# A streaming encoder step: gate and z projections in pairs by seven block products, in a stage of their own

## Chip, cores and metric

The kernel runs on one core of a Trainium2 chip. The metric is device time in microseconds of one launch, inputs and outputs in device memory. One core has five engines that each run their own list of instructions in program order: TensorE (PE, matrix products into PSUM), VectorE (DVE), ScalarE (ACT), GpSimd (POOL) and SyncE (SP, which issues most transfers).

## What is computed

One layer of an encoder for 512 prompt tokens and 64 sample tokens (576 columns in all), width 2048, fp32. Cut to what matters:

```python
h = RMSNorm(x) * (1 + scale) + shift
[gdn q|k|v, gdn z, gdn beta, gdn a, att q, att k, att v, att z,
 idx q, idx k, idx w, gate_a, gate_b] = h @ W_in
A = W_bA( GatedRMSNorm(GatedDeltaRule(silu(conv4(qkv)))) * silu(z_A) )
B = W_bB( SparseAttn_topk(indexer) * silu(z_B) )
x = x + gate * W_out( sigmoid(gate_a) * A + sigmoid(gate_b) * B )
```

The delta rule has 16 heads of 128 x 128 state, walked in chunks of 64 tokens with a triangular solve per chunk. The indexer scores keys for each token, and only the 256 best take part in the attention (16 heads, 2 key heads, 1024 cached keys for the sample). Outputs are y, the new keys, values and indexer keys, and the new delta-rule and convolution states.

## The kernel before

**Tiles.** Almost all of PE's time goes into the products of h (576 columns, held on chip, transposed, as a high part `hh` and a low part `hl`) with weight matrices, 128 weight columns at a time. Such a *tile* takes 96 matmuls: 16 blocks of the inner dimension, two halves of 288 tokens, and three products each (high x high, high x low, low x high) that together stand for one fp32 product. These are the matmuls with a 128x288 operand, here called wide. `run_tile` and `half` (L292) run one. While tile n runs, `load` (L261) brings the weights of tile n+3 by one 1 MB transfer of SP, and `split` (L273) makes the high part of tile n+1's weights (`whi`, a copy on ACT) and the low part (`wlo`: ACT writes the negated high part, and a transfer of POOL's queue adds the raw weights to it). At the end of each half a tile's epilogue runs: for a gate tile tanh on ACT (`gth`, `gate_epi` L1459) and a store to device memory (`d_t`); for a z tile tanh and a product on DVE (`gz`, `za_epi` L1512) and a store (`d_za`).

**Order.** `plan` (L1668) writes the list of tiles. Everything else (convolution, solve, scan, attention, top-k) is written as generators, the *tasks*. While the program is built, `tick` follows each matmul and lets the tasks that are due put in their next instructions; due times come from a book-keeping of the engines in the planner. So tasks' instructions lie between those of the tiles, and each engine's list is fixed when the kernel is built. A tile may have a function to run ahead of it (`pre`): `q_pre(h)` (L1237) does `join` on the scan of head h-2, `qb_pre` (L1408) joins attention tasks, and `open_gdn`, `open_att`, `open_ga` change the memory pools and join what is left. A `join` puts in all the instructions of a task up to its end with no tile matmul between them.

**Stages.** Keys kb0, kb1, then `misc` (indexer keys, beta, a), eight indexer-query tiles qi0 to qi7 with the score products, values vb0 and vb1, seven gates g00 to g06 during which DVE does the top-k (`topks` L886: 16 rounds each for three prompt blocks, 32 rounds for the sample, one MAX8 and one MATCH_REPLACE per round). Then the delta rule: for each head tiles c0, c1, c2 (its q, k, v; c02 is q of head 2) with 12 z tiles and 9 gates among them, 4.3 tiles per head in the mean. Per head: convolution (`conv` L912), products kk, steps on M (`solve` L1059; the block `dN` goes through a transfer first), products z and y, then the scan (`scan` L1146) with state S and products pks, px, pS, po, a norm on DVE, and transposes oTp, oTq of the result ot. Three more gates, then 16 pairs of tiles qb, zb with attention (`attend` L1306), two gates after zb7, four z tiles, eight gates g18 to g115 under which `load_ga` brings oa and za from device memory (`ga<-oa`), then the branch products ya, yb and wo.

Of the kernel before, what the change touches and what calls it, by code (L numbers as in the profile page):

```python
# [16 lines left out]
D = 2048  # L17
KO = 16
# [9 lines left out]
MARK = -3e38  # L28


O_QA, O_ZA, O_BA, O_QB, O_KB, O_VB, O_ZB, O_QI, O_KI, O_GA, O_GB = (
# [174 lines left out]
class Kern(Plan):  # L206
# [51 lines left out]
    def win(self, name, c, epi, pre=None, n=128):  # L258
        self.add(name, [(self.i["w_in"][0], c, n)], lambda: self.h, epi, pre)

    def load(self, n):  # L261
        if n >= len(self.stream):
# [4 lines left out]
        r3 = raw[:, :KO * m].rearrange("p (k m) -> p k m", m=m)  # L267
        at = 0
        for src, c, w in d["srcs"]:
            self.S.dma_start(r3[:, :, at:at + w], src[:, c:c + w].rearrange("(k p) m -> p k m", p=128))  # L270
            at += w

    def split(self, n, q, of=4, eng=None):  # L273
        if n >= len(self.stream):
            return
        d = self.stream[n]
        if q == 0:
            d["hi"] = self.wp.tile([128, 2048], F32R, tag="whi", name=f"whi{n}")
            d["lo"] = self.wp.tile([128, 2048], F32R, tag="wlo", name=f"wlo{n}")
        w = KO * d["m"] // of  # L280
        s = slice(w * q, w * q + w)
        self.A.activation(d["hi"][:, s], d["raw"][:, s], AF.Copy)
        if eng:
            eng.tensor_tensor(d["lo"][:, s], d["raw"][:, s], d["hi"][:, s].bitcast(F32), op=ALU.subtract)
            return

        self.A.activation(d["lo"][:, s], d["hi"][:, s].bitcast(F32), AF.Copy, scale=-1.0)
        if q % 2:
            s = slice(w * q - w, w * q + w)
            self.G.dma_start(d["lo"][:, s], d["raw"][:, s], accum_op=ALU.add)  # L290

    def half(self, n, s, ps, ks, hook=None, part=None):  # L292

        d = self.stream[n]
        m = d["m"]
        hi = d["hi"][:, :KO * m].rearrange("p (k m) -> p k m", m=m)
        lo = d["lo"][:, :KO * m].rearrange("p (k m) -> p k m", m=m)
        ah, al = d["act"]()
        sl = slice(288 * s, 288 * s + 288)
        i = 0  # L300
        for k in ks:
            for j, (w, x) in enumerate(((hi, ah), (hi, al), (lo, ah))):
                if part is not None and part != j // 2:
                    continue
                self.mm(ps[:m, :288], w[:, k, :], x[:, k, sl], start=k == 0 and j == 0, stop=k == KO - 1 and j == 2)
                i += 1
                if hook:
                    hook(i)
                self.tick()

    def run_tile(self, n):
        d = self.stream[n]
        if d["pre"]:
            d["pre"]()

        count = [0]

        def hook(_):
            i = count[0] = count[0] + 1
            if i in (4, 14, 24, 34):  # L320
                self.split(n + 1, (i - 4) // 10)
            if i == 84:
                self.load(n + 3)

        ps = {}
# [17 lines left out]


    def consts(self, ctx):
# [4 lines left out]
        self.mE = cp.tile([128, 2, 128], F32, name="mE")  # L350
        self.ones = cp.tile([128, 1], F32, name="ones")
# [6 lines left out]
        dt = self.dp.tile  # L358
        self.d_g = dt([16, TX], F32, name="d_g")
        self.d_kT = dt([2, 128, T], F32, name="d_kT")  # L360
        self.d_v = dt([T, 256], F32, name="d_v")
# [77 lines left out]
    def start(self, ctx, hctx):  # L439
# [9 lines left out]
        with tc.tile_pool(name="x0", bufs=2, side="right", reuse_waits="tile") as xp:  # L449
# [16 lines left out]
            for t in range(5):  # L466
# [6 lines left out]
                    self.rows_load(xp, [s[0:96]], "s0", S), self.rows_load(xp, [s[96:144]], "s1", S)]  # L473
            S.dma_start(self.mE, i["k_mask"])
            S.dma_start(self.diag, i["k_diag"])
# [177 lines left out]
    def misc(self):  # L653
        i, o, p, A, V, G, mT = self.i, self.o, self.p1, self.A, self.V, self.G, self.mT
        cp = self.cp
        yield [mT]

        for a, b, at in ((0, TP, 0), (TP, T, TP + PAST)):
            c = slice(at, at + b - a)
            A.activation(self.kih[0:64, c], mT[0:64, a:b], AF.Copy)  # L660
            A.activation(self.kih[64:128, c], mT[0:64, a:b], AF.Copy)
            for x, R in enumerate((slice(0, 64), slice(64, 128))):
                V.tensor_tensor(self.kil[R, c] if at else self.kiz[R, x, :], mT[0:64, a:b], self.kih[0:64, c].bitcast(F32), op=ALU.subtract)
        mt = p.tile([128, 5, 112], F32, name="mt", bufs=1)
# [78 lines left out]
        yield [self.d_g]  # L743

    def cache_idx(self):
        i, p = self.i, self.p1
# [70 lines left out]
    def score(self, m, qi, qs):  # L817
# [4 lines left out]
        else:  # L822
            yield from self.wait(self.misc_task, self.cache_task)
        units = []
# [634 lines left out]
    def gate_epi(self, b, j):  # L1459
        def epi(ps, s):  # L1460
            if s == 0:
                p = self.gpool()
                n = 2 if p is self.p2 else 1
                self.room(p, n)
                self.gth = p.tile([128, T], F32, tag="gth", name=f"gth{b}{j}", bufs=n)
            th = self.gth
# [201 lines left out]
    def plan(self):  # L1668
        self.stream = []
        w = self.i["w_in"][0]  # L1670
        for which, col in (("k", O_KB), ("v", O_VB)):
            for n in range(2):
                self.win(f"{which}b{n}", col + 128 * n, self.kv_epi(which, n))
            if which == "k":
                self.add("misc", [(w, O_KI, 80), (w, O_BA, 32)], lambda: self.h, self.misc_epi)
                for m in range(8):
                    self.win(f"qi{m}", O_QI + 128 * m, self.qi_epi(m))
        gates = [(b, j) for b in range(2) for j in range(KO)]
# [14 lines left out]

        gate(1)
        gate(6, self.open_gdn)
        for h in range(H):
            for j, g in (((1, 0), ) if h == 0 else ()) + ((0, h), (2, h)) + (((1, h + 1), ) if h < 15 else ()):
                self.win(f"c{j}{g}", 2048 * j + 128 * g, self.conv_epi(j, g), (self.q_pre(g), self.head_pre(g), None)[j])
            z(1) if h % 4 else gate(1)
            if h < 4:  # L1700
                gate((3, 1, 0, 0)[h])
            if h % 4 == 3:
                gate(1)
# [21 lines left out]
    def drain(self):  # L1725
        while self.tasks:
            self.join(*self.tasks)

    def open_gdn(self):
# [3 lines left out]
        self.c2, self.p2 = self.pool("p2")  # L1733
        self.slack = 0.0
        self.gpool = lambda: self.p2
# [52 lines left out]
    def run(self):  # L1788
        tc = self.tc
        with ExitStack() as ctx:  # L1790
# [10 lines left out]
            self.score_tasks, self.topk_task = [], None  # L1801
            self.topk_gap, self.solve_gap, self.gada_gap = 100, 0, 5000
            self.plan()
            self.hctx = ExitStack()
            pss = self.start(ctx, self.hctx)
            self.catt, self.ap = self.pool("att", bufs=1)
            self.msk = [self.ap.tile([128, 128 * t + 128], F32, name=f"msk{t}") for t in range(4)]
            self.msks = self.ap.tile([128, NS], F32, name="msks")
            self.c1, self.p1 = self.pool("p1")
            self.gpool, self.p2 = lambda: self.p1, None  # L1810
            p = self.p1
            self.kih, self.kil = (p.tile([128, TP + NS], F32R, name=n, bufs=1) for n in ("kih", "kil"))

            self.kiz = p.tile([128, 2, TP], F32R, name="kiz", bufs=1)
            for x, R in enumerate((slice(64, 128), slice(0, 64))):
                self.V.tensor_scalar(self.kiz[R, x, :].rearrange("p (a b) -> p a b", b=128),
                                     self.ident[R].unsqueeze(1).to_broadcast([64, 4, 128]), 0.0, None, op0=ALU.mult)
            self.qss = []
            for b in range(2):
                q = p.tile([128, 2, 128], F32R, name=f"qss{b}", bufs=1)  # L1820
                self.V.tensor_scalar(q, self.ident.unsqueeze(1).to_broadcast([128, 2, 128]), 0.0, None, op0=ALU.mult)
                self.qss.append(q)
            self.tri = p.tile([128, 2, 128], F32, name="tri", bufs=1)
            self.cache_task = self.spawn(self.cache_idx())
            self.load(3)
# [4 lines left out]
            self.load(4)  # L1830
            for n in range(2, len(self.stream) - 2):
                self.run_tile(n)
# [63 lines left out]
```

## Time and profile before

| | us |
|---|---|
| median of three runs | 3089.07 |
| lowest and highest | 3082.39, 3091.2 |
| the profiled execution | 3076.14 |
| its span in the trace | 3074.4 |

A row of a group view gives an operation as output<-inputs, its shape, the count, busy time, the mean of one in ns, and what ended the idle time before it. In a strip, each digit is the busy share of one fortieth of the span in tenths. A row of a timeline gives start, duration, engine, line, operation, count and, in brackets, the idle time before it and what released it. The granted clock (PEclk) is given as a share of full speed, 2.4 GHz.

### The profile page before, as it was taken

How to read it: one execution, taken by the hardware profiler on the slowest of the kernel's cores; microseconds unless marked ns; L12 is line 12 of the kernel's file. 1: busy time of each engine (PE TensorE's matmuls, PEld its weight loads, DVE VectorE, ACT ScalarE, POOL GpSimd, SP SyncE). 2: the span in 40 equal slices, each digit the busy share in tenths (PEclk: the TensorE clock that was granted, in tenths of full speed). 3: DMA queues.
4: the chain of work that ended last, by engine and by line, in shares of the span. 5: the costliest groups of instructions: out<-in, count | busy, mean ns of one | idle time of the engine just before them, and what ended most of it. 6: DMA issues, size and time to landing. Idle time of an engine off the chain costs nothing.

```text
span 3074.4 us, 56422 instructions
## 1 busy us (share of the span) xinstructions
PE 2949.8 (96%) x22363; PEld 2811.9 (91%) x22363; DVE 1389.5 (45%) x4059; ACT 1542.1 (50%) x3332; POOL 390.6 (13%) x727
## 2 busy tenths in 40 slices
PE   6999999999999999999998799999999999999897
PEld 2599999999999989999997799899999999999897
DVE  3344997666567657666641344344412111111112
ACT  3266445565555556665553355445544444444454
POOL 1001111111111111111110011011111111111110
PEclk7999999999999999999998899999999999999999
DMA  9865887766666666677667767776769899888875
GB/s 327 279 157 124 196 184 178 159 154 155 142 149 145 151 146 148 148 172 161 156 151 155 163 167 171 188 171 160 174 152 250 220 240 237 215 203 223 215 161 140
DMA packets 567242, 552.40 MB, mean 180 GB/s; under 512 B 53505, under 2 KB 466066, under 8 KB 565762
## 3 DMA queue, kind: packets, MB, share of 16 engines
q1 hardware_dynamic: 512690, 351.58, 40.5%
q0 software_dynamic: 54144, 197.16, 33.7%
q8 instruction: 176, 2.88, 0.4%
q14 instruction: 88, 0.72, 0.1%
q10 hardware_dynamic: 144, 0.07, 0.0%
HBM read 303.54 MB, written 48.04 MB: 114 GB/s over the span
## 4 chain that ended last, share of the span: by engine, by line
PE 78%; DMA 11%; SPq 3%; ACT 3%; DVE 3%; issue 2%; POOL 0%; ACTq 0%; DVEq 0%; POOLq 0%
PE mm L218 63%; SPq L55 3%; DMA za<-d_za 2%; DMA wlo<-wraw 2%; DMA gbl<-d_gb 1%; PE ada L218 1%; PE ob L218 1%; DMA wa<-in_w_ada 1%; PE lg L218 1%; PE po L218 1%; PE dot L218 1%; ACT wlo L55 1%; PE mmp L218 1%; DMA xf<-in_x_sample 1%; ACT whi L55 1%
## 5 line engine op out<-in xcount | busy, mean ns | idle before, releaser
L218 PE MATMUL mm<-hh,whi 128*128 128x288 f32 (+1 forms) x4448 | 1221.0, 301 | 4.5 <-ACT gth L55 4.2
L218 PE MATMUL mm<-hl,whi 128*128 128x288 f32 (+1 forms) x4448 | 1218.3, 300 | 0.0
L218 PEld LDWEIGHTS mm<-hh,whi 128*128 128x128 f32 (+1 forms) x4448 | 839.6, 189 | 18.1 <-issue 7.8
L218 PEld LDWEIGHTS mm<-hl,whi 128*128 128x128 f32 (+1 forms) x4448 | 840.1, 189 | 10.2 <-issue 6.1
L218 PE MATMUL mm<-hh,wlo 128*128 128x288 f32 (+1 forms) x4448 | 682.5, 303 | 4.8 <-DMA wlo<-wraw 4.8
L218 PEld LDWEIGHTS mm<-hh,wlo 128*128 128x128 f32 (+1 forms) x4448 | 618.2, 191 | 11.5 <-DMA wlo<-wraw 5.1
L55 POOL DMA_DIRECT2D wlo<-wraw x376 | 324.5, 863 | 2311.4 <-ACT wlo L55 2035.2
L55 ACT ACTIVATE wlo<-whi 128x512 fp32r<-128x512 f32 x752 | 475.8, 633 | 81.1 <-PE mm L218 46.1
L55 ACT ACTIVATE whi<-wraw 128x512 fp32r<-128x512 f32 x756 | 467.9, 619 | 78.4 <-DMA wraw<-in_w_branch_b 27.5
L55 DVE TENSOR_TENSOR Mt<-M 18x30 f32<-18x30 f32 (+14 forms) x480 | 151.7, 316 | 31.2 <-DMA M<-dN 21.9
L55 DVE TENSOR_TENSOR M<-M,Mt 18x30 f32<-18x30 f32 (+14 forms) x480 | 153.6, 320 | 16.7 <-DVE Mt L55 0.3
L218 PE MATMUL mm<-ga,whi 128*128 128x288 f32 x1024 | 140.9, 297 | 6.1 <-DVE ta L55 5.0
L218 PE MATMUL mm<-mg,whi 128*128 128x288 f32 x1024 | 144.9, 299 | 0.0
L218 PEld LDWEIGHTS mm<-ga,whi 128*128 128x128 f32 x1024 | 138.2, 190 | 7.0 <-DVE ta L55 5.7
L218 PEld LDWEIGHTS mm<-mg,whi 128*128 128x128 f32 x1024 | 139.5, 190 | 0.0
L218 PE MATMUL mm<-gb,whi 128*128 128x288 f32 x1024 | 138.6, 295 | 0.0
L218 PEld LDWEIGHTS mm<-gb,whi 128*128 128x128 f32 x1024 | 136.8, 188 | 0.0
L55 DVE SCALAR_TENSOR_TENSOR cv<-raw,cw,cv 128x579 f32<-128x579 f32 x144 | 117.4, 815 | 4.3 <-ACT cv L55 0.8
L55 DVE SCALAR_TENSOR_TENSOR gacc<-gada,cs,gacc 128x512 f32<-128x512 f32 x120 | 86.7, 745 | 31.4 <-DMA gada<-in_w_ada 31.4
L55 ACT ACTIVATE x<-px 128x128 f32<-128x128 f32 (+1 forms) x80 | 22.0, 275 | 149.2 <-PE px L218 149.2
L55 ACT ACTIVATE raw<-mm 128x288 f32<-128x288 f32 x96 | 36.7, 382 | 99.0 <-PE mm L218 98.2
L55 DVE TENSOR_TENSOR xf<-yp,xf 128x512 f32<-128x512 f32 (+1 forms) x18 | 11.4, 633 | 161.9 <-PE yp L233 134.8
(478 smaller groups left out, 3298.7 us busy)
## 6 DMA issues: line engine op xcount, KB each, us to landing
wlo<-wraw POOLq DMA_DIRECT2D x376, 512.0 KB, 5.4
wraw<-in_w_in SPq DMA_DIRECT2D x140, 1024.0 KB
wa<-in_w_ada SPq DMA_DIRECT2D x64, 512.0 KB
gada<-in_w_ada SPq DMA_DIRECT2D x64, 256.0 KB
wraw<-in_w_branch_a SPq DMA_DIRECT2D x16, 1024.0 KB
wraw<-in_w_branch_b SPq DMA_DIRECT2D x16, 1024.0 KB
wraw<-in_w_out SPq DMA_DIRECT2D x16, 1024.0 KB
d_t<-gth SPq DMA_DIRECT2D x32, 288.0 KB
```

The costliest lines, as they stand in the source:

```text
L55: r = f(*a, **k)
L218: self.nc.tensor.matmul(out, lhsT, rhs, start=start, stop=stop, **k)
```

## The change

28 tiles, 16 of the 32 gates and 12 of the 16 z tiles, are taken out of the list and put into a stage of their own. Two neighbouring tiles make a pair: a product of a 2 x 2 block matrix (two groups of 128 weight columns by two halves of the inner dimension) with another (two halves of the inner dimension by two halves of tokens). Written out that is 8 block products of 24 wide matmuls; the new code forms seven, on sums and differences of the blocks (a scheme of the Strassen-Winograd kind). The sums of weight blocks and their low parts are made on DVE (`prep`, `parts`), the sums of the token blocks once for all pairs (`tblocks`: four blocks T, high and low), and seven additions on DVE join the products (`post`). ACT makes the high parts; no accumulating transfer is used there.

The stage stands behind g00 to g05 and ahead of the indexer: kb, misc, vb, six gates, 14 pairs, then qi0 to qi7, two gates, the delta rule with three tiles per head (four z tiles are left, after heads 3, 7, 11 and 15), three gates, qb and zb without gates between, and five gates g111 to g115 under `load_ga`. The weights' buffers become halves of 512 KB, two per tile.

```diff
+PLAN = (6, 12, 10)
-        raw = d["raw"] = self.wp.tile([128, 2048], F32, tag="wraw", name=f"wraw{n}")
+        for b in range(2):
+            raw = self.wblock("wraw", f"wraw{n}_{b}")
...
+    def tblocks(self):
+        for k in range(8):
+            for n, (kk, t) in enumerate(((k, 0), (k, 1), (k + 8, 0), (k + 8, 1))):
+                V.tensor_tensor(u[n], f(hh[:, kk, sl]), f(hl[:, kk, sl]), op=ALU.add)
+            V.tensor_tensor(t[5], u[1], u[0], op=ALU.subtract)
...
+            for x in (5, 7, 6, 4):
+                A.activation(self.TB[x][0][:, k, :], t[x], AF.Copy)
+            for x in (5, 7, 6, 4):
+                V.tensor_tensor(self.TB[x][1][:, k, :], t[x], f(self.TB[x][0][:, k, :]), op=ALU.subtract)
+    def parts(self, p, x, src):
+        for q in range(2):
+            self.A.activation(hi[:, s], src[:, s], AF.Copy)
+        for q in range(2):
+            self.V.tensor_tensor(lo[:, s], src[:, s], hi[:, s].bitcast(F32), op=ALU.subtract)
+    def prep(self, p, step):
+        if step == "A":
+            self.parts(p, 1, a[0, 0])
+            tt(a[1, 0], a[1, 0], a[1, 1], ALU.add)
...
+    def run_pair(self, p, last):
+            elif x == 6:
+                tt(st["b"], st["a"], ps[6])
+            elif x == 5:
+                tt(st["c"], st["b"], ps[5])
...
+        order = (1, 6, 5, 4, 7, 2, 3)
+            for k in range(8):
+                for j, (w, y) in enumerate(((hi, bh), (hi, bl), (lo, bh))):
+                    self.mm(o, w[:, k, :], y[:, k, :], start=k == 0 and j == 0, stop=k == 7 and j == 2)
...
         for h in range(H):
-            z(1) if h % 4 else gate(1)
-            if h < 4:
-                gate((3, 1, 0, 0)[h])
-            if h % 4 == 3:
-                gate(1)
+            if zs and (h + 1) * (16 - nz) // 16 > h * (16 - nz) // 16:
+                z(1)
         gate(3)
         for h in range(H):
             self.win(f"zb{h}", O_ZB + 128 * h, self.zb_epi(h))
-            if h == 7:
-                gate(2)
```

How the lists of instructions change is shown at three places. In them a name such as mm31_1 is tile 31 of the list, half 1; 0 in oTp0 or TT0 is the head; S02 and po03 are head 0, chunks 2 and 3.

PE, before, at the end of the scan of head 0, where the transposes oTp0 and oTq0 of its result stand:

```order
L218 MATMUL mm31_0_5945<-hh_99,wlo31_5721 128x288 x16
L218 MATMUL mm31_1_6018<-hh_99,wlo31_5721 128x288 x6
L233 MATMUL oTp0_0_6106<-ident_60,ot0_5551 128x128 x4
L218 MATMUL mm31_1_6018<-hh_99,wlo31_5721 128x288
L233 MATMUL oTq0_0_6113<-ident_60,ot0_5551 128x64
L218 MATMUL mm31_1_6018<-hh_99,wlo31_5721 128x288 x9
```

and now, up to the first matmul of tile c02 (mm28):

```order
L221 MATMUL pks03_0_9388<-S02_9379,k0_8059 128x128
L221 MATMUL po03_9387<-S02_9379,q0_8303 128x128
L221 MATMUL px03_0_9398<-r03_9391,TT0_8145 128x128
L221 MATMUL pS03_0_9402<-x03_9400,kd0_8477 128x128
L221 MATMUL po03_9387<-x03_9400,e10_7870 128x128
L236 MATMUL oTp0_0_9457<-ident_60,ot0_9285 128x128 x4
L236 MATMUL oTq0_0_9463<-ident_60,ot0_9285 128x64
L221 MATMUL mm28_0_9471<-hh_99,whi28_0_8897 128x288
```

The whole solve products and scan of head 0 stand ahead of c02 without a wide matmul among them.

DVE, before, at the last top-k round of the sample: it lies among the solve steps M0 of head 0, ahead of all copies Z0, TT0 and S0 of that head:

```order
L55 MAX max8s31_4991<-msks_1027 64x8
L55 MATCH_REPLACE msks_1027<-max8s31_4991,msks_1027 64x1088
L55 TENSOR_TENSOR Mt0_4557<-M0_4459 18x184
L55 TENSOR_TENSOR M0_4459<-M0_4459,Mt0_4557 18x23x8
L55 TENSOR_SCALAR msks_1027<-msks_1027 64x1088 x2
```

and now, rounds 20 to 22 of 32 between the copies of head 0 that PE waits for:

```order
L58 MAX max8s20_9224<-msks_5969 64x8
L58 MATCH_REPLACE msks_5969<-max8s20_9224,msks_5969 64x1088
L58 COPY Z0_9227<-z00_0_9228 32x128 x2
L58 COPY Z0_9227<-z00_0_9228 32x32
L58 MAX max8s21_9241<-msks_5969 64x8
L58 MATCH_REPLACE msks_5969<-max8s21_9241,msks_5969 64x1088
L58 COPY TT0_8145<-z10_0_9244 32x4x32 x2
L58 COPY TT0_8145<-z10_0_9244 32x32
L58 MAX max8s22_9262<-msks_5969 64x8
```

The rounds have moved into the stretch in which head 0's solve and scan run.

PE, before, behind the scan of head 4 (pS43, po43), and the transposes of its result further on, 103 wide matmuls later:

```order
L218 MATMUL pS43_0_9593<-x43_9558,kd4_8836 128x128
L218 MATMUL po43_9539<-x43_9558,e14_8081 128x128
L218 MATMUL mm48_1_9569<-hh_99,whi48_9265 128x288
L218 MATMUL mm48_1_9569<-hl_100,whi48_9265 128x288
L218 MATMUL mm48_1_9569<-hh_99,whi48_9265 128x288
```

```order
L218 MATMUL mm49_1_9785<-hh_99,whi49_9509 128x288
L233 MATMUL oTp4_0_9818<-ident_60,ot4_9240 128x128 x4
L218 MATMUL mm49_1_9785<-hl_100,whi49_9509 128x288
L233 MATMUL oTq4_0_9827<-ident_60,ot4_9240 128x64
L218 MATMUL mm49_1_9785<-hh_99,whi49_9509 128x288
```

and now:

```order
L221 MATMUL mm40_1_12493<-hh_99,wlo40_1_12222 128x288 x8
L221 MATMUL pS43_0_12645<-x43_12612,kd4_11766 128x128
L221 MATMUL po43_12587<-x43_12612,e14_11251 128x128
L236 MATMUL oTp4_0_12709<-ident_60,ot4_12279 128x128 x4
L236 MATMUL oTq4_0_12719<-ident_60,ot4_12279 128x64
L221 MATMUL mm41_0_12732<-hh_99,whi41_0_12421 128x288
```

No wide matmul stands between the scan's last product and the transposes any more.

## Rows read from the trace of the kernel before

**Rows 1.** The page: busy time of each engine, and strips of PE and DVE.

```profile
PE 2949.8 (96%) x22363; PEld 2811.9 (91%) x22363; DVE 1389.5 (45%) x4059; ACT 1542.1 (50%) x3332; POOL 390.6 (13%) x727
...
PE   6999999999999999999998799999999999999897
...
DVE  3344997666567657666641344344412111111112
```

**Rows 2.** The chain of waits: start, us, what; one of its longest pieces.

```profile
2900.40 12.73 PE mm L218 x96
```

**Rows 3.** Stretches: us, busy PE, PEld, DVE, ACT, POOL, clock, DMA share, GB/s.

```profile
446.04:1533.78 1087.74, 1068.69 (x8675) 1026.66 (x8674) 727.15 (x2366) 625.21 (x1382) 166.04 (x441) 0.99 0.68 155
320.00:430.00 110.00, 110.00 (x834) 110.00 (x833) 101.97 (x188) 50.44 (x93) 15.89 (x22) 1.00 0.83 195
```

**Rows 4.** The same view of the wide matmuls (tile mm) alone; PE comes first.

```profile
446.04:1533.78 1087.74, 938.47 (x6383) 864.78 (x6382) 19.05 (x66) 51.57 (x134) 0.99 0.68 155
```

**Rows 5.** The page's costliest groups: the products with low parts.

```profile
L218 PE MATMUL mm<-hh,wlo 128*128 128x288 f32 (+1 forms) x4448 | 682.5, 303 | 4.8 <-DMA wlo<-wraw 4.8
```

**Rows 6.** Groups by line and form, on DVE and ACT.

```profile
L55 ACT ACTIVATE whi<-wraw 128x512 fp32r<-128x512 f32 x752 | 465.9, 620 | 76.1 <-DMA wraw<-in_w_branch_b 27.5 <-PE mm L218 18.6 <-DMA wraw<-in_w_branch_a 10.8
...
L55 ACT ACTIVATE gth<-mm 128x288 f32<-128x288 f32 x64 | 25.9, 406 | 110.5 <-PE mm L218 103.0 <-DMA d_t<-gth 7.3
...
L55 DVE TENSOR_TENSOR oa<-oa,za 128x288 f32<-128x288 f32 x32 | 14.6, 456 | 42.0 <-DMA za<-d_za 42.0
...
L55 DVE TENSOR_TENSOR xf<-xf,fw 128x512 f32<-128x512 f32 x14 | 9.7, 693 | 23.8 <-ACT fscr L55 21.4 <-DMA fw<-in_final_norm_w 2.3
```

**Rows 7.** Tiles max8p and max8s: ns min/median/max, first and last start, forms.

```profile
L55 DVE MAX8 max8p<-msk x48: 391/561/697, 310.8 to 371.5; 128x8 f32<-128x256 f32 x16, 128x8 f32<-128x384 f32 x16, 128x8 f32<-128x512 f32 x16
...
L55 DVE MATCH_REPLACE8 msk<-max8p,msk x48: 407/542/678, 311.3 to 372.3; 128x256 f32<-128x256 f32 x16, 128x384 f32<-128x384 f32 x16, 128x512 f32<-128x512 f32 x16
...
L55 DVE MAX8 max8s<-msks x32: 1271/1284/1287, 373.3 to 496.9; 64x8 f32<-64x1088 f32 x32
L55 DVE MATCH_VALUE_LOAD msks<-max8s,msks x32: 83/83/85, 374.6 to 498.3; 64x8 f32 x32
L55 DVE MATCH_REPLACE8 msks<-max8s,msks x32: 1266/1268/1270, 374.7 to 498.3; 64x1088 f32<-64x1088 f32 x32
```

**Rows 8.** Timeline of DVE in the last head's scan, two steps of the state.

```profile
1625.93 0.35 DVE L55 SCALAR_TENSOR_TENSOR S<-S,egl,pS 128x128 f32<-128x128 f32 x1 [2.56 <-PE pS L218]
...
1630.50 0.35 DVE L55 SCALAR_TENSOR_TENSOR S<-S,egl,pS 128x128 f32<-128x128 f32 x1 [2.31 <-PE pS L218]
```

**Rows 9.** Timeline of PE at the end of that scan.

```profile
1630.30 0.39 PE L218 MATMUL po<-x,e 128*128 128x128 f32 x2
...
1636.78 1.35 PE L233 MATMUL oTp<-ident,ot 128*128 128x128 f32 x4 [3.73 <-ACT ot L55]
```

**Rows 10.** Timeline of DVE: the first solve step of two heads in a row.

```profile
698.14 0.18 DVE L55 TENSOR_TENSOR Mt<-M 18x30 f32<-18x30 f32 x1
...
761.14 0.19 DVE L55 TENSOR_TENSOR Mt<-M 18x30 f32<-18x30 f32 x1 [0.69 <-DMA M<-dN]
```

**Rows 11.** Timeline of DVE at the end of the attention.

```profile
2248.91 0.46 DVE L55 SCALAR_TENSOR_TENSOR zt<-zt,mm 128x288 f32<-128x288 f32 x1 [1.66 <-ACT zt L55]
...
2288.86 0.36 DVE L55 SCALAR_TENSOR_TENSOR gb<-obs,zt 128x64 f32<-128x64 f32 x2 [5.35 <-PE obs L218]
```

**Rows 12.** Timeline of DVE: first and last product under the gates behind the attention.

```profile
2316.30 0.46 DVE L55 TENSOR_TENSOR oa<-oa,za 128x288 f32<-128x288 f32 x1 [4.90 <-DMA za<-d_za]
...
2410.75 0.46 DVE L55 TENSOR_TENSOR oa<-oa,za 128x288 f32<-128x288 f32 x1 [1.76 <-DMA za<-d_za]
```

**Rows 13.** Stretches behind two stops of PE, columns as in rows 3.

```profile
841.37:848.60 7.23, 7.23 (x27) 6.07 (x28) 2.87 (x10) 1.53 (x4) 0.00 (x0) 0.50 0.20 42
1712.37:1715.60 3.23, 3.23 (x12) 3.05 (x13) 2.18 (x9) 0.10 (x1) 0.00 (x0) 0.50 0.83 219
```

**Rows 14.** Timeline of PE at the second of these stops.

```profile
1712.37 1.22 PE L218 MATMUL lg<-KT,qT 128*128 128x256 f32 x2 [17.09 <-DVE L L55]
```

More of the change, by code (lines that the diff above doesn't have):

```diff
@@ L304, in half @@
                     continue
-                self.mm(ps[:m, :288], w[:, k, :], x[:, k, sl], start=k == 0 and j == 0, stop=k == KO - 1 and j == 2)
+                self.mm(ps[:m, :288], w[k // 8][:, k % 8, :], x[:, k, sl], start=k == 0 and j == 0, stop=k == KO - 1 and j == 2)
                 i += 1
@@ L323, in hook @@
                 self.load(n + 3)
+            if n == self.edge - 1:
+                if i == 1:
+                    for w in ((0, 0), (1, 1), (0, 1), (1, 0)):
+                        self.pair_load(0, w)
+                if i == 50:
+                    self.prep(0, "A")
+                if i == 70:
+                    self.prep(0, "B")
         ps = {}
@@ new lines, in pair_load @@
+    def pair_load(self, p, which):
+        if p >= len(self.pairs):
+            return
+        i, j = which
+        n = self.nraw = self.nraw + 1
+        t = (self.ts.tile([128, 1024], F32, tag="wx", name=f"wx{p}{i}{j}") if n % 5 == 0 else self.wblock("wraw", f"wp{p}{i}{j}"))
+        c = self.pairs[p]["col"] + 128 * i
+        self.S.dma_start(t.rearrange("p (k m) -> p k m", m=128),
+                         self.i["w_in"][0][1024 * j:1024 * j + 1024, c:c + 128].rearrange("(k p) m -> p k m", p=128))
+        self.pairs[p]["A"][i, j] = t
@@ new lines, in pair_out @@
+    def pair_out(self, p, which, x, done):
+        A, V, ts, d = self.A, self.V, self.ts, self.pairs[p]
+        i, t = which
+        sl = slice(288 * t, 288 * t + 288)
+        kind, b, j = d["to"][i]
+        if kind == "gate":
+            A.activation(done, x, AF.Tanh, scale=0.5)
+            dst = self.d_t[b, j]
+        else:
+            e = ts.tile([128, 288], F32, tag="se", name=f"e{p}{i}{t}")
+            A.activation(e, x, AF.Tanh, scale=0.5)
+            V.scalar_tensor_tensor(done, e, 1.0, x, op0=ALU.add, op1=ALU.mult)
+            dst = self.d_za[j]
+        return self.spawn(self.store(dst[:, sl], done))
@@ new lines, in run_pairs, with last @@
+    def run_pairs(self, after):
+        def last(x):
+            if x == 7:
+                self.edge = 1 << 30
+                self.load(after)
+                self.load(after + 1)
+            elif x in (2, 3):
+                for q in ((0, 1) if x == 2 else (2, 3)):
+                    self.split(after, q)
+        self.posts = []
+        self.join(self.tb_task)
+        self.room(self.ts, 1)
+        self.pair_load(1, (0, 0))
+        for p in range(len(self.pairs)):
+            self.run_pair(p, last if p == len(self.pairs) - 1 else None)
+        for f in self.posts:
+            f()
+        self.load(after + 2)
+        self.drain()
+        self.cts.close()
+        self.ctb.close()
@@ L743, in misc, with keys_idx @@
         yield [self.d_g]
+    def keys_idx(self):
+        A, V = self.A, self.V
+        mT = self.p1.tile([64, T], F32, name="kiT", bufs=1)
+        self.S.dma_start(mT, self.d_ki)
+        yield [mT]
+        for a, b, at in ((0, TP, 0), (TP, T, TP + PAST)):
+            c = slice(at, at + b - a)
+            A.activation(self.kih[0:64, c], mT[:, a:b], AF.Copy)
+            A.activation(self.kih[64:128, c], mT[:, a:b], AF.Copy)
+            for x, R in enumerate((slice(0, 64), slice(64, 128))):
+                V.tensor_tensor(self.kil[R, c] if at else self.kiz[R, x, :], mT[:, a:b], self.kih[0:64, c].bitcast(F32), op=ALU.subtract)
     def cache_idx(self):
@@ L822, in score @@
         else:
-            yield from self.wait(self.misc_task, self.cache_task)
+            yield from self.wait(self.keys_task, self.cache_task)
         units = []
@@ L1805, in run @@
             pss = self.start(ctx, self.hctx)
[L1806 to L1824, printed above, removed]
+            self.c1, self.p1 = self.pool("p0")
+            self.gpool, self.p2, self.ts = lambda: self.p1, None, 0
+            self.tri = self.p1.tile([128, 2, 128], F32, name="tri", bufs=1)
             self.load(3)
@@ L1830, in run @@
             self.load(4)
-            for n in range(2, len(self.stream) - 2):
+            for n in range(2, self.nA):
+                self.run_tile(n)
+            self.run_pairs(self.nA)
+            for n in range(self.nA, len(self.stream) - 2):
                 self.run_tile(n)
```

201 lines of the change are left out of this document (169 added, 32 removed).

## The prediction

> **What bounds the kernel now.** The page was read first: TensorE (PE) is busy 96% of the span, and the strip of 40 slices shows it full almost from end to end [rows 1]. The chain of waits has hardly anything but PE's 288-column matmuls, 22,363 PE instructions in all [rows 1, 2]. One such matmul costs 12.73 us / 96 = 0.1326 us in a row of them [rows 2]. So before, time goes as PE work, and a saved matmul is a saved 0.1326 us, but only as long as PE has something to run while the other engines work. That is the point to look at. VectorE (DVE) is at 45% over the span, yet not evenly: 102.0 of 110 us in the top-k stretch, 727 of 1088 us through the delta rule, while PE there is at 98% to 100% [rows 3]. Those engines' work is hidden behind the z and gate tiles that the change takes away.
>
> **What is removed.** 14 pairs x 8 products x 24 matmuls become 14 x 7 x 24: 336 matmuls fewer. 336 x 0.1326 = **-44.6 us**. This can't go further, since no other PE work falls away. The accumulating DMAs of these tiles' low parts go too, but PE lost only 4.8 us to those in the whole kernel [rows 5], so I count nothing (ends 0 and -5).
>
> **The new stage by itself.** Per pair PE has 168 x 0.1326 = 22.3 us. DVE has four 128x1024 sums, fourteen 128x512 subtractions at 0.69 us (nearest row: a product of that shape), seven 128x288 sums at 0.46 and for six of the pairs two z products of about the same [rows 6]: the sums, taken as two 128x512 each, are 8 x 0.69, so (8 + 14) x 0.69 + 7 x 0.46 + 1 = 19.4 us. ACT has 14 copies of 128x512 at 0.62 = 8.7 us and a few of 0.41 [rows 6]. So DVE is 87% loaded, PE stays the bound, and the cost is 0; if adds of two PSUM or fp32 operands go up to 3 us over PE per pair, 14 x 3 = 42 is the other end. Before the first block the token blocks T are formed by about 100 DVE instructions; 24 of them and 9 of ACT stand in a join with no matmul beside them: 24 x 0.3 + 2 = **+9** (0 to 20; block 1 needs none of them).
>
> **What is moved.** Engines work in program order, so the order decides which stretches have tiles to fill. In the new order several joins stand with no 288-column matmul ahead of PE's next step:
>
> (a) *Tile c02, which waits for the scan of head 0.* Before, the 80 top-k rounds ran under the q tiles and gates. Now they stand in DVE's queue among the steps of head 0's solve and scan, 31 of the 32 sample rounds ahead of or between the copies that PE waits for, and PE has between the last tile and c02 only head 0's small products. DVE: 48 prompt rounds at (0.561 + 0.083 + 0.542) and 32 sample rounds at (1.284 + 0.083 + 1.268) = 56.9 + 84.3 = 141 us [rows 7], and 1.6 heads at 727.15 / 15 = 48.5 us [rows 3], 78: 219. At the density of DVE in the top-k stretch of before, 101.97 / 110 = 93% [rows 3], that is 236; PE has 760 wide matmuls between the first round and c02, 100.8 us, and 1.6 heads' small products, per head (1068.69 - 6383 x 0.1326) / 15 = 14.8 [rows 3, 4]; together 124.5. The difference is 112; with the two marks of the scores, **+113** (95 if DVE is gapless, 130).
>
> (b) *Tile c03*: all of scan 1 (27 PE instructions, 77 DVE) without cover. Five chunks at 4.6 us (the step from S at 1625.93 to S at 1630.50, [rows 8]) and a tail of 6.5, less 5.6 of PE work: **+23** (12 to 30). Before c04 a part of one: **+5** (0 to 10).
>
> (c) *Nine heads, before c05, c06, c07, c09, c010, c011, c013, c014 and c015.* Three tiles are left per head: 288 x 0.1326 + 14.8 = 53.0 us of PE work, where before a head took 1087.74 / 15 = 72.5 [rows 3]. Between the scan's last product and the transposes of its result stood 76 to 105 wide matmuls by the order; now none. From that product (1630.30) to the transposes (1636.78) the one uncovered case of before took 6.5 us [rows 9], and now twelve solve steps of 0.4 us stand on DVE ahead of the norm: about 8.5, and one or two more where the next solve, thus later, is awaited. I take 10 each, **+90**. For it speaks the shortest step of before from one solve to the next, 63.0 us (698.14 to 761.14, [rows 10]), 10 over 53.0. Ends: 6 each (54), and 18.5 each (166) if the head period stays 72.5 - 1. Heads 3, 7, 11 and 15 keep a z tile: 65.7 us of PE work, nothing lost.
>
> (d) *Attention.* The z and gate tiles also stood around tile qb8 and ahead of g111. qb0: 2.5 more scan chunks uncovered, **+12**. qb8 and g111 now each wait for an attend block and a sample block (45 to 53 PE instructions) with nothing beside them. From the gating tile to the product with it, that chain took 39.95 us (2248.91 to 2288.86, [rows 11]) with filler, 8 of them its own PE work; without queueing behind filler I take 30 - 8 = 22 each, **+44** (15 to 32 each).
>
> (e) *The loads of z and oa before ya0* are used from 2316.30 to 2410.75, 94.5 us, and DVE waits for transfers at both ends [rows 12]. Eight gates covered that (8 x 96 x 0.1326 = 102 us); five are left, 64 us, so 31 are open; with three tiles' weights fewer on the queues I take **+22** (10 to 40).
>
> (f) *The clock.* Behind one stop of PE the granted clock was 0.50 for 7.23 us, and behind one of 17.09 us for 3.23 us [rows 13, 14], that is 1.2 in place of 2.4 GHz: 3.6 and 1.6 us lost. Seven large stops x 2.6 = **+18** (0 to 50).
>
> **Against that** the stops of before that vanish where they were: PE's idle 1087.74 - 1068.69 = 19 us in the delta rule [rows 3] and about 8 of half clock: **-27**.
>
> The Trainium skill has a rule that bears on (f): "TensorE: Matmul & The Clock Gate", Part 1, makes the throttled clock the default and full speed what activity earns, so every one of some 16 stops would resume at 1.2 GHz; at the 3.6 us of the longer row that would be about 58 us in place of 18, and the total 3380. Row and rule agree that a stop is followed by the lower level; how much time that takes is here known from two stops alone, so I keep 18 and put the rest into the range.
>
> **Sum:** -44.6 + 9 + 113 + 23 + 5 + 90 + 12 + 44 + 22 + 18 - 27 = **+264**. Against the profiled execution (3076.14, its span 3074.4) that is 3340; the median of the runs, 3089.07, is 13 higher, so I say **3350**.
>
> **Rivals.**
>
> 1. *The stops don't occur* and the change is faster. Each stop is a wait of PE for the slowest of other engines; if DVE, without the filler's epilogues, is far enough ahead that chains end before PE arrives, only -44.6 and the pair stage are left: 3089 - 44.6 = 3044. The point from which it decides: all stops together below 44.6 us. For it: DVE idles 55%. Against it: the stretch up to c02 alone holds 219 us of DVE work against 124.5 of PE work, and no wait can make DVE shorter. Its half way, within 0.3% of before, needs the stops at 35 to 54 us. On this the skill speaks too ("TensorE: Matmul & The Clock Gate", Part 2): matmuls keep program order, and only weight loads are pulled ahead. The trace agrees: PE stood 17.09 us on L with tile matmuls queued behind it [rows 14].
>
> 2. *Only the top-k stop bites*: head chains shrink with the filler to nearly PE's work (tails of 4 us) and attention's stops halve. -44.6 + 9 + 113 + 12 + 40 + 12 + 22 + 10 + 10 - 27 = +156: 3245.
>
> 3. *The new stage is bound by DVE or its loads*, not PE: +42 on the sum, about 3390. For it: DVE at 87% and sums that no row shows in this shape. Against it: each is needed a whole block ahead.
>
> 4. *The head period stays* at about 72 us, because DVE's solve chain is the clock and not PE: 18.5 in place of 10 per head, 3350 + 76 = 3426. Against it: DVE has only 48.5 us of work per head.
>
> That the change doesn't save what it says isn't open: the order has 17,808 wide matmuls for 18,144.
>
> **How the numbers follow.** Main case 0.50, rival 4 0.18, rival 2 0.13, rival 3 0.12, rival 1 0.04, and within 0.3% 0.03 (0.3%, 9 us, is about what a measurement of this kernel can tell from no change). All low ends together: -50 + 95 + 12 + 54 + 12 + 30 + 10 - 27 = +136, 3225; all high ends give over 3550, not likely together. The range 3225 to 3440 leaves out 2 in 10, rival 1 and the sums of several high ends. Faster 0.04, same 0.03, slower 0.93.
>
> **What would show it.** Right: in the new trace one stretch of some 100 us ahead of c02 with PE almost idle and DVE above 90%; a gap of 8 to 10 us ahead of the transposes of heads 4, 5, 6, 8 and on; gaps of some 20 us ahead of qb8, g111 and ya0; a pair stage at 14 x 22.3 = 312 us with PE at 98%. Wrong: PE above 95% over the whole span (rival 1); gaps under 4 us per head (2); DVE above 95% in the pair stage (3); heads 72 us apart (4).

## The result and the profile after

The changed kernel takes 3327.58 us (median, 3325.89 to 3333.39) against 3085.78 before, a ratio of 1.0786 (95% interval 1.077 to 1.0803): 242 us slower, where 264 were forecast. The profiled execution spans 3324.1 us against 3074.4.

The page of the changed kernel: its span, busy times, and the strips of PE and of the granted clock.

```profile
span 3324.1 us, 57075 instructions
...
PE 2980.1 (90%) x22027; PEld 2817.5 (85%) x22027; DVE 1651.8 (50%) x4505; ACT 1539.6 (46%) x3350; POOL 343.7 (10%) x671
...
PE   6999999899448988988988887998999889999998
...
PEclk8999999999758998999999988998999989999999
```

336 PE instructions fewer than in [rows 1], as said, and yet PE is busy 30 us longer. What lies outside its busy time went from 124.6 us (3074.4 - 2949.8) to 344.0 (3324.1 - 2980.1): 219.4 us of new idle time. The rest is the clock. Summed over the time in which PE was busy, the clock record of the trace has 204.5 us at half speed against 83.8 before, which costs (204.5 - 83.8) / 2 = 60 us. So the work itself, counted at full clock, did fall: 30.3 - 60.3 = -30 us. The three together give the 249.7 by which the spans differ. The 336 matmuls are worth 44.6 us; what the 15 us between the two may be is taken up with the four-pair kernel below. The strip shows the deepest hole in the eleventh and twelfth slice (4, 4, with the clock at 7 and 5); then 8 and 9 alternate up to the twenty-fourth, where before 9 stood.

PE's waits in the changed kernel: who waited for what, us in total, times, longest.

```profile
PE oTp L236 <- ACT ot L58: 100.3, 13, 8.4
PE z L221 <- DMA TT<-dX: 70.2, 15, 58.8
PE lg L221 <- DVE L L58: 22.8, 6, 18.0
PE mm L221 <- ACT ga L58: 13.3, 5, 4.1
PE cikp L236 <- DMA cik<-in_cache_idx_k: 12.1, 1, 12.1
PE px L221 <- DVE r L58: 11.6, 8, 3.0
```

The first two hold 170 us, where before they held 7. `oTp` are the transposes behind each head's scan (3.7 us before, in one wait, [rows 9]), `z` the first product after the solve (3.3 us before, in eight waits). The timeline of PE shows both at their places: ahead of the products of head 0, and behind the scan of head 3 and on into the next tile.

```profile
870.41 0.27 PE L236 MATMUL vbq<-ident,raw 128*64 128x128 f32 x1
929.52 0.28 PE L221 MATMUL z<-TT,e 32*32 32x32 f32 x2 [58.84 <-DMA TT<-dX]
...
1176.91 0.39 PE L221 MATMUL po<-x,e 128*128 128x128 f32 x2
1185.72 1.35 PE L236 MATMUL oTp<-ident,ot 128*128 128x128 f32 x4 [8.42 <-ACT ot L58]
...
1188.18 0.44 PE L221 MATMUL mm<-hl,whi 128*128 128x288 f32 x1
1188.42 0.44 PE L221 MATMUL mm<-hh,whi 128*128 128x288 f32 x1
```

Nine heads have the second stop, each 8.42 or 8.43 us long; the matmuls behind it start 0.24 us apart, not 0.13. Stretches of the changed kernel (columns as in rows 3): the pair stage, from the first product kk to oTp of head 0, the rest of the delta rule, the attention, and the 6.6 us behind the stop above.

```profile
268.90:599.50 330.60, 320.13 (x2356) 316.43 (x2355) 242.96 (x391) 138.60 (x276) 0.85 (x1) 0.99 0.43 115
795.90:979.57 183.67, 92.83 (x688) 85.66 (x686) 176.88 (x394) 51.63 (x113) 15.38 (x43) 0.71 0.31 70
979.57:1964.18 984.61, 875.80 (x6946) 821.26 (x6946) 670.25 (x2260) 525.78 (x1209) 133.06 (x386) 0.93 0.57 127
2039.41:2601.20 561.79, 532.15 (x3745) 501.34 (x3746) 227.50 (x692) 263.93 (x571) 49.98 (x58) 0.95 0.65 153
1185.72:1192.30 6.58, 6.58 (x26) 5.90 (x27) 5.34 (x16) 4.13 (x8) 0.00 (x0) 0.50 0.34 80
```

In the second stretch DVE is busy for 176.88 of 183.67 us (96%) and PE for 92.83: DVE has become the bound there. In the third PE is idle for 109 us. Before, the same two places (from oTp of head 0 to that of head 15; the attention) read:

```profile
582.30:1636.78 1054.48, 1031.42 (x8397) 987.55 (x8394) 666.09 (x2246) 606.49 (x1358) 158.09 (x416) 0.99 0.67 154
1712.37:2288.50 576.13, 570.19 (x4159) 544.72 (x4160) 229.57 (x696) 288.07 (x616) 57.81 (x67) 0.99 0.70 166
```

So the delta rule became only 70 us shorter although 1451 PE instructions were taken out of it.

### The profile page after: what moved, and what is told of

Its sections match the earlier page's. It is cut to its first block, busy times and chain, and to the rows that moved or that the text cites. A ratio compares the mean times of both kernels' runs of the same rounds, so it can differ in the third digit from the quotient of the medians.

```text
span 3324.1 us, 57075 instructions
## 1 busy us (share of the span) xinstructions
PE 2980.1 (90%) x22027; PEld 2817.5 (85%) x22027; DVE 1651.8 (50%) x4505; ACT 1539.6 (46%) x3350; POOL 343.7 (10%) x671
## 5 line engine op out<-in xcount | busy, mean ns | idle before, releaser
L221 PE MATMUL mm<-hh,whi 128*128 128x288 f32 (+1 forms) x3552 | 1000.5, 307 | 1.9 <-ACT gth L58 1.9
L221 PE MATMUL mm<-hl,whi 128*128 128x288 f32 (+1 forms) x3552 | 994.2, 305 | 0.0
L221 PEld LDWEIGHTS mm<-hh,whi 128*128 128x128 f32 (+1 forms) x3552 | 688.4, 194 | 15.9 <-issue 7.4
L221 PEld LDWEIGHTS mm<-hl,whi 128*128 128x128 f32 (+1 forms) x3552 | 688.2, 194 | 8.6 <-issue 5.3
L221 PE MATMUL mm<-hh,wlo 128*128 128x288 f32 (+1 forms) x3552 | 544.0, 302 | 3.9 <-DMA wlo<-wraw 3.9
L221 PEld LDWEIGHTS mm<-hh,wlo 128*128 128x128 f32 (+1 forms) x3552 | 492.4, 190 | 7.4 <-DMA wlo<-wraw 4.1
L58 ACT ACTIVATE wlo<-whi 128x512 fp32r<-128x512 f32 x640 | 404.4, 632 | 142.4 <-PE mm L221 103.8
L58 ACT ACTIVATE whi<-wraw 128x512 fp32r<-128x512 f32 (+1 forms) x644 | 398.0, 619 | 45.9 <-PE mm L221 34.7
L221 PE MATMUL mm<-ga,whi 128*128 128x288 f32 x1024 | 143.9, 300 | 13.4 <-ACT ga L58 13.3
L58 DVE TENSOR_TENSOR plo<-wp,phi 128x512 fp32r<-128x512 f32 x158 | 101.2, 687 | 26.0 <-ACT phi L58 25.5
L58 ACT ACTIVATE phi<-wp 128x512 fp32r<-128x512 f32 x158 | 88.6, 619 | 50.5 <-DVE wp L58 50.5
L236 PE MATMUL oTp<-ident,ot 128*128 128x128 f32 x64 | 19.2, 428 | 100.3 <-ACT ot L58 100.3
```

The source lines that it names most:

```text
L58: r = f(*a, **k)
L221: self.nc.tensor.matmul(out, lhsT, rhs, start=start, stop=stop, **k)
L236: self.nc.tensor.transpose(out, in_, self.ident[:k, :k])
```

## The experiments

The theory: the time comes from where the tiles stand, not from the seven products. PE now meets joins with nothing to run, because the tiles that stood there have gone into the pair stage. Rivals: the new stage itself is what costs, or the period of a head is set by a chain of the other engines that no tile can shorten.

### Move without scheme, and scheme without the top-k

The first kernel has the changed order, with the 28 tiles left as plain tiles of eight products.

```diff
-        gate(n0 - 2, self.open_pairs)
+        gate(n0 - 2)
...
+        for (d, c) in todo:
+            epi = self.gate_epi(d[1], d[2]) if d[0] == "gate" else self.za_epi(d[2])
+            self.win("t", c, epi)
...
-            self.run_pairs(self.nA)
```

> The changed kernel's order with its 28 tiles left as plain tiles of eight products: the move without the scheme. Theory (the time comes from the order, the seven products save PE work): the stops of the changed kernel stay in place, 59 us ahead of the first products z of head 0 and nine of 8.4 us ahead of oTp; the stage of tiles costs 28 x 96 x 0.1326 = 356 us where the pairs took 330.6, so about 3327 + 26 = 3353, 1.087 times before. Rival (the new stage and what it does to DVE and the pools is what costs): without it the time falls back to within 1% of before, 3085 to 3115.

Measured: 3348.73 us, 1.0861 (1.0836 to 1.0887). The move alone costs 263 us, and the scheme gives back 3348.7 - 3327.6 = 21 of the 44.6 that its matmuls are worth. PE's waits in it are those of the changed kernel:

```profile
PE oTp L236 <- ACT ot L58: 100.5, 13, 8.5
PE z L221 <- DMA TT<-dX: 78.9, 17, 58.6
```

The rival on the stage falls. Then the changed kernel without the sample's top-k rounds:

```diff
-        yield from self.topk(self.msks[:64, :], 256, "s")
+        yield ("dve", 100)
+        self.topk_out(self.msks[:64, :])
```

> The changed kernel without the 32 top-k rounds of the sample (part of the computation left out; the marks are then made from the unreduced scores). Theory (these rounds hold DVE ahead of tile c02): the idle of 58.8 us ahead of z of head 0 goes, and the steps between z and oTp of head 0 lose about 2.6 us each, in all 75 to 95 us less: 3235 to 3250. Rival (head 0's own solve and scan are the wait, the rounds only stand beside it): under 30 us less, above 3295.

Measured: 3265.56 us, 62 less: below the 75 to 95 expected and far above the rival's 30. PE's longest wait for TT falls from 58.8 to 20.4 us (columns of the waits as above):

```profile
PE z L221 <- DMA TT<-dX: 37.2, 19, 20.4
```

The stretch from kk to oTp of head 0 shrinks from 183.7 to 129.6 us, 54, and PE's idle time in it from 90.8 to 36.8. So about 6 tenths of this stop are the sample's rounds. What is left is not the latency of head 0's own solve and scan alone: the 48 prompt rounds are still in this kernel and run among head 0's solve steps up to 863 us (its kk starts at 794.5), and with all rounds spread out (below) only 20.7 us of idle time stay in this stretch. The same place can be mended without leaving work out: eight gates (four pairs fewer) go between the indexer and the delta rule.

```diff
-PLAN = (6, 12, 10)
+PLAN = (6, 12, 18)
...
-        gate(2)
+        gate(10)
         first = self.open_gdn
```

> The changed kernel with eight gates (four pairs fewer) put between the indexer and the delta rule, as cover for the top-k alone; heads and attention as changed. Theory (the rounds hold PE ahead of c02 for want of tiles): the stop of 58.8 us ahead of z of head 0 and the rounds between its steps go, some 30 us of head 0's bare scan stay, as they did without the sample rounds; four pairs cost 4 x 24 matmuls back, 13 us: 3327 - 60 + 13 = 3280 (3265 to 3295). Rival (rounds and head 0 are bound to each other by the planner's due times, not by room): the 90 us stay, 3330 to 3345.

Measured: 3270.18 us. 57 us are won although eight products replace seven in four pairs. PE's idle time from kk to oTp of head 0 is 30.5 us (90.8 in the changed kernel). The longest wait for TT is 14.3 us, and that for oTp is where it was:

```profile
PE oTp L236 <- ACT ot L58: 97.9, 12, 8.4
PE z L221 <- DMA TT<-dX: 36.5, 19, 14.3
```

### A tile for each head

Eight pairs; the 12 z tiles go back into the delta rule, so that each head has one.

```diff
-PLAN = (6, 12, 10)
+PLAN = (6, 0, 10)
```

> Eight pairs in place of 14: the 12 z tiles go back into the delta rule, one per head, in place of three heads in four without one. Theory (one tile per head covers the end of the scan): all nine stops of 8.4 us and the half clock behind each (3.3 us) go, 105 us, the stops of c02 and c03 stay or lose some 5; six pairs fewer give back 6 x 24 = 144 matmuls, 19 us, less the waits of the z pairs for tanh (7 us): 3327 - 105 + 12 = about 3235. Rival (the head period is set by DVE's chain): heads stay 65 us or more apart beyond the added tile's 12.7 us, time 3300 or above.

Measured: 3200.17 us, 127 less, more than the 92 expected. The delta rule behind head 0:

```profile
833.46:1832.22 998.76, 966.52 (x7905) 920.35 (x7905) 678.86 (x2280) 579.55 (x1309) 150.46 (x406) 0.99 0.66 149
```

and PE's waits:

```profile
PE z L221 <- DMA TT<-dX: 45.2, 17, 36.6
...
PE oTp L236 <- ACT ot L58: 22.8, 3, 8.8
```

959 PE instructions more are ten of the twelve tiles, 10 x 96 x 0.1326 = 127 us of PE work, and the stretch grows from 984.6 to 998.8, by 14. The z tiles run there almost for nothing; in the pair stage, where 28 tiles took 330.6 us, ten of them take 118 us. The clock is back at 0.99. The stop ahead of c02 became shorter too (36.6 for 58.8): two z tiles more, 25 us of PE work, stand ahead of it now.

### Is it the join, or the chain behind it?

The end of the scan (norm, transposes, store) becomes a task of its own, so that the join ends with the scan's last product.

```diff
         self.drop("po")
+        self.spawn(self.scan_out(st, ot))
+
+    def scan_out(self, st, ot):
```

> The changed kernel with the end of the scan (norm, scaling, transposes, store) made a task of its own, so that tile c0 of head h+2 waits for the scan's last product only. Theory (the wait for the norm is the cost): nine stops of 8.4 us and the half clock behind them go, 105 us: 3222. Rival (the chain from solve to solve sets the head period, and the wait moves to the scan's own steps, which now stand without tiles): heads come 60 us or more apart where they were 65 to 68, and under 45 us are gained, above 3280.

Measured: 3375.25 us, 48 slower than the changed kernel. The stops of 8.4 us are gone, and shorter waits have come in their place (the delta rule behind head 0 as a stretch):

```profile
984.95:2012.48 1027.53, 925.51 (x6835) 840.70 (x6833) 663.27 (x2238) 524.40 (x1192) 137.26 (x376) 0.88 0.54 119
```

and the two that grew among PE's waits:

```profile
PE px L221 <- DVE r L58: 45.9, 40, 3.0
PE pS L221 <- ACT x L58: 26.9, 66, 0.7
```

With the join earlier, the planner puts the last chunks of the scan themselves ahead of the tile, without a wide matmul among them. The idle time stays about as it was (1027.53 - 925.51 = 102 us for 109), the clock falls to 0.88 from 0.93, and that is most of the difference: by the clock record PE was busy for 189 us at half speed in this stretch, where it had been 86. Over the whole execution it is 304 us for 204, which costs 50 of the 62 us by which PE's busy time grew; the other 12 are not explained by the clock. Neither theory had this; the rival (the wait moves into the scan) is right on the place.

The second test fills the stops with work that nobody reads: 60 wide matmuls behind the scan of each of the nine heads.

```diff
         self.drop("po")
+        if h in (3, 4, 5, 7, 8, 9, 11, 12, 13):
+            for _ in range(60):
+                self.nc.tensor.matmul(po[:, 128:416], self.h[0][:, 0, 0:128], self.h[0][:, 0, 0:288], start=True, stop=True)
```

> The changed kernel with 60 more 288-column matmuls on PE (into an unused part of the scan's PSUM tile, read by nobody) behind the scan of each of the heads 3, 4, 5, 7, 8, 9, 11, 12, 13, where PE stands still for 8.4 us: 540 matmuls more. Theory (a stop costs its idle time and then a stretch at 1.2 GHz): the matmuls fit into the stops, the granted clock behind them stays at 1.0, and the 3.3 us of half clock per head go: 3327 - 30 = 3297. Rival (the half clock has another cause than the stop, or the stop's price is its idle time alone): no change or slower, 3325 to 3360; if the matmuls did not fit, up to 540 x 0.1326 = 72 us slower.

Measured: 3343.80 us, 16 slower, not 30 faster; its interval (1.0793 to 1.0879 of before) just meets that of the changed kernel (1.077 to 1.0803). The theory missed. The timeline of PE in the same head as above:

```profile
1181.05 8.17 PE L1413 MATMUL po<-hh 128*128 128x288 f32 x60 [0.37 <-ACT ot L58]
1189.13 1.21 PE L236 MATMUL oTp<-ident,ot 128*128 128x128 f32 x4
...
1207.74 0.67 PE L221 MATMUL z<-TT,e 32*32 32x32 f32 x16 [3.39 <-DMA TT<-dX]
```

and the stretch from its oTp on, columns as in rows 3 (the clock is third from the end):

```profile
1189.10:1198.50 9.40, 9.40 (x66) 8.68 (x66) 7.04 (x21) 6.86 (x12) 0.00 (x0) 1.00 0.26 79
```

The matmuls fit, and the clock behind them stays at 1.00, as the theory said. But the 3 us that the next tiles win are lost again at `z`, which now waits 3.39 us for the solve of that head (its result comes back through a transfer, dX), and at the lower clock behind that wait. Without the filling that wait was 0.5 to 2.1 us in the nine heads, with it 2.6 to 3.9. So a second chain, from solve to solve, seems to stand close behind the first; taking one stop away only shows it.

### The top-k spread over the heads

The pause that the planner keeps between two rounds goes from 100 to 8000 ns.

```diff
-            self.topk_gap, self.solve_gap, self.gada_gap = 100, 0, 5000
+            self.topk_gap, self.solve_gap, self.gada_gap = 8000, 0, 5000
```

> The changed kernel with the top-k rounds spread out: the pause that the planner keeps between two rounds goes from 100 to 8000 ns, so that the last sample round stands under head 10 and not ahead of c02. Theory (DVE's work has no room to go: heads of three tiles leave it 65.7 - 48.5 = 17 us idle, but the tails hang on its order): the idle between kk and oTp of head 0, 90.8 us, falls to 35 to 50, and the heads up to 10 grow by 2 to 5 us each, so 3327 - 50 + 30 = about 3305 (3285 to 3330). Rival (DVE's idle time takes the rounds for nothing): heads stay at 65 to 68 us and the whole 50 us and the half clock behind it are gained, 3260 to 3275.

Measured: 3309.99 us, within the theory's range. From kk to oTp of head 0 it takes 114 us for 184, with 20.7 us of idle time for 90.8, but the delta rule behind it 1043.7 for 984.6:

```profile
791.90:906.17 114.27, 93.60 (x695) 86.73 (x693) 85.43 (x284) 51.58 (x113) 15.73 (x43) 0.85 0.51 115
906.17:1949.87 1043.70, 887.79 (x6945) 824.30 (x6946) 783.62 (x2443) 529.04 (x1209) 132.85 (x386) 0.90 0.53 120
```

PE's wait for the end of the scan, 100.3 us in the changed kernel:

```profile
PE oTp L236 <- ACT ot L58: 120.3, 14, 11.2
```

Of 70 us won at one place 59 are lost at the other. DVE is at 75% there and can't take 113 us more, although a quarter of its time is free: its rounds of 2.6 us stand ahead of the steps that PE waits for.

### Pairs from spare tiles only

Two kernels put the tiles back where PE stood still, and make pairs of gates alone. The first (seven pairs) also spreads the rounds, and uses the cached indexer keys 12 us later.

```diff
+        n0, nz, np = 4, 0, 7
...
+            z(1)
+            gate({0: 2}.get(h, 0))
...
+            if h == 7:
+                gate(2)
```

> Seven pairs of gates only, and the tiles put back where PE stood still: one z tile in each head, two gates behind head 0, two behind zb7, four gates ahead of the stage; the top-k rounds spread (8000 ns), and the first use of the cached indexer keys put 12 us later, where PE waited 12 us for their transfer. Theory (the stops are the whole cost, the scheme itself saves what it says): nearly all stops go; against the kernel before 7 x 24 = 168 matmuls, 22 us, are saved, less 6 us at the start of the stage and some 10 us at the uncovered scan of head 10 and ahead of ya: 3075, between 3065 and 3095. Rival (the stage or the new buffers cost something the stops don't show): 3110 or above.

Measured: 3162.32 us, 1.025 (1.0222 to 1.0277): far outside 3065 to 3095, and in the rival's range. In the delta rule the spread rounds do the same harm as above, and the start of the pair stage, with two gates fewer ahead of it, waits for the token blocks:

```profile
730.10:1793.07 1062.97, 994.91 (x7964) 941.85 (x7962) 788.55 (x2451) 583.33 (x1312) 151.30 (x411) 0.96 0.63 142
```

and two of PE's waits:

```profile
PE oTp L236 <- ACT ot L58: 48.2, 11, 10.5
...
PE P L221 <- ACT T6h L58: 11.9, 4, 3.1
```

The second (four pairs) keeps the rounds close together, under seven gates.

```diff
+        n0, nz, np = 6, 0, 4
...
-        gate(2)
+        gate(7)
...
+            z(1)
+            gate({0: 3, 1: 1}.get(h, 0))
...
+            if h == 7:
+                gate(2)
```

> Four pairs of gates; all other tiles back as cover: seven gates ahead of the delta rule for the top-k (rounds at 100 ns as before), one z tile per head, three gates behind head 0 and one behind head 1, two behind zb7, two ahead of ya; cached indexer keys used 12 us later. Theory (cover is the whole cost, and DVE has room for the rounds only there): no long stop is left, heads 67 to 70 us apart; 4 x 24 = 96 matmuls, 12.7 us, are saved, the start of the new stage costs some 8 us, the shorter cover ahead of ya 5 to 15: 3075 to 3100, within 0.5% of before. Rival (the stage costs something beyond stops): 3110 or above.

Measured: 3122.34 us, 1.0111 (1.0092 to 1.0131). 205 of the 242 us are back, but it is still slower than before, 22 us above the theory's range and in the rival's. What is left of waits:

```profile
PE mm L221 <- ACT ga L58: 25.6, 12, 4.3
PE lg L221 <- DVE L L58: 22.0, 5, 19.3
PE z L221 <- DMA TT<-dX: 16.2, 22, 1.8
PE oTp L236 <- ACT ot L58: 10.0, 2, 5.7
```

`ga` (the products under the last gates, of which two are left for eight) waits 25.6 us, where the changed kernel had 13.3. PE's idle time is 160.7 us in all (124.6 before) and its busy time at half clock 109 us (83.8), 36 and 13 us; the 96 saved matmuls are 12.7. The two profiled executions are 46.3 us apart, so 10 us stay open. Counted the same way, the changed kernel has 15 us open (what the -30 above lacks of -44.6), and the kernel with 28 plain tiles has 8 without a single pair (265 us more span than before, of which 213.5 are idle time and 43 the clock). So at least a part of this rest is no cost of the pairs. What it is was not tested; the new weight buffers, which all these kernels share, are not ruled out. No version with pairs came out ahead of the kernel before.

## Why the prediction was right

The sign, the places and the sizes of the two largest terms held, the smaller terms did not. By its terms (idle time read at the place, the clock in a line of its own):

| term | forecast | measured |
|---|---|---|
| seven products, the new stage | -44.6 + 9 | -26: 330.6 us for 28 x 12.73 = 356.4 |
| (a) c02 | +113 | +91 idle, 10 of half clock |
| (b) c03, c04 | +28 | +10 |
| (c) nine heads | +90 | +76: 9 x 8.43 |
| (d) qb0 | +12 | about 0 |
| (d) qb8, g111 | +44 | +24: idle 29.6 for 5.9 in the attention |
| (e) ya0 | +22 | +8: waits for ga 13.3 for 5.0 |
| (f) clock, all of it | +18 | +60 |
| first use of the cached indexer keys | none | +12 |
| idle of before that vanishes | -27 | about 0: 109 us idle in the delta rule are (b), (c) and 22 of other waits, for 23 before |

*Terms that held.* (a): DVE was the bound of the stretch, at 96%, with the rounds between the steps of head 0; without the sample's rounds its 91 us of idle time became 36.8, with eight gates as cover 30.5, with the rounds spread 20.7. So at least 70 of the 91 us are the rounds, and at most 21 the head's own latency. (c): the nine stops are at the scans of heads 3, 4, 5, 7, 8, 9, 11, 12 and 13, which the tiles named in (c) wait for (the list of signs names heads one too high). The tail costs 8.43 us, near the 8.5 worked out from [rows 9] and the twelve solve steps; the one or two us of awaited solve came too, as 0.5 to 2.1 us ahead of z. The shortest step of [rows 10], 63.0 us, was no chain's limit: by the same measure, from the first solve step of one head to that of the next, the changed kernel once takes 58.4 us.

```profile
1033.56 0.19 DVE L58 TENSOR_TENSOR Mt<-M 18x30 f32<-18x30 f32 x1 [0.18 <-DMA M<-dN]
...
1092.01 0.19 DVE L58 TENSOR_TENSOR Mt<-M 18x30 f32<-18x30 f32 x1
```

The heads behind it come 65.0 to 68.1 us apart, and some 67 with one z tile in each. The plan of the kernel before has 12 gates in the delta rule, not 9, so 4.5 tiles per head; the sum for (c) takes its period from the trace and doesn't change by it.

*Terms that failed.* (f) was too small by a factor of three. I scaled two stops of before and took seven large ones, though I had counted some 16; the short tails cost their clock as well: behind the 8.42 us at 1185.72 the granted clock was 0.50 for 6.6 us. The clock record has 32 stretches at half speed, where before it had 16. The Trainium skill's rule in "TensorE: Matmul & The Clock Gate", Part 1, by which the lower clock is the default and full speed is what activity earns, gave 58 us in the prediction, as an estimate for some 16 stops; the trace agrees with 60. It was the better step to sum by. (The total of 3380 that stands beside it is counted from the profiled execution; counted as the forecast of 3350 is, it would be 3390.)

(d) and (e) were too high: the attention's block chain stops PE for 12.2 us in all at qb8 and 10.2 at g111, not 22 each, and the five gates ahead of ya0 nearly cover the loads (only with two left, in the four-pair kernel, the wait for ga reaches 25.6 us). (b) was taken for a whole bare scan, and only the tail was bare. The 12 us wait for the cached keys was in no term: their load moved behind the pairs with the pool that holds it, a move of a transfer that I had not priced. The -27 was wrong too: it counted the waits of before as gone, and others came in their place. The new stage lost 19 us of its 44.6, where I had 9: some 3 us of waits at the start, about 3 for the half clock behind them, and 1.4 us in each of five pairs of z tiles. There the product with tanh waits for ACT, and on DVE it stands ahead of the sum of weight blocks that the next product needs:

```profile
479.19 0.46 DVE L58 SCALAR_TENSOR_TENSOR sa<-e,sa 128x288 f32<-128x288 f32 x1 [0.57 <-ACT e L58]
479.56 1.22 DVE L58 TENSOR_TENSOR wp<-wx,wp 128x1024 f32<-128x1024 f32 x1
```

That makes 13 of the 19; the other 6 were not placed.

*The rivals.* The first (stops don't occur) is out with 219.4 us of idle time. The second (only the top-k) is out with nine tails at 8.43. The third, the stage bound by DVE, is out: PE was busy 97% of it, DVE 73%. The fourth (heads 72 us apart) is out as a period, 984.6 / 15 = 65.6, but the filled stops point to a chain from solve to solve close behind. That the total came within 22 us is in part luck, errors that cancel: the clock, the cached keys, the new stage and the idle time of before were together 91 too low (42, 12, 10, 27), (a) to (e) 100 too high (22, 18, 14, 32, 14).

## What to carry to other kernels

A matmul that runs while PE would otherwise wait for other engines costs next to nothing, and making it cheaper saves next to nothing; moving it away costs its cover. So ahead of any change that saves work by regrouping it, list what each piece covers where it stands, and draw only on pieces that cover nothing: here ten z tiles cost 14 us in the delta rule and 118 us in a stage of their own. That such a choice wins is not shown here: the kernel with four pairs of gates was still 37 us slower than before. When one stop is filled, look for the next chain behind it before counting the gain.

## What the runs showed of the hardware

Many short waits cost more here than fewer, longer ones of about the same sum. With 102 us of idle time in waits of under 6 us the mean granted clock of the delta rule was 0.88; with 109 us, of which 76 in nine stops of 8.4 us, it was 0.93; with a z tile in each head, 32 us idle, 0.99. The time at half speed (189 us of PE's busy time for 86), not the idle time, made the first stretch 43 us longer than the second (1027.5 for 984.6).
